# Rounding the query and output weights ahead, and four smaller moves, in a fused decoder block

## The chip, the cores and the metric

The kernel runs on one core of a Trainium2 chip. The metric is device time in microseconds for one execution. Of the kernel before there are three runs, with a median of 2021.86 us, from 2018.86 to 2024.74. A difference of under 0.3%, some 6 us, can't be told from no change by such runs.

Five engines work at the same time, each through its own list of instructions, in order: TensorE (PE: matrix products and transposes), VectorE (DVE), ScalarE (ACT), GpSimd (POOL) and SyncE (SP), which here only issues transfers between DRAM and on-chip memory. ScalarE can issue transfers too. Engines wait for one another through semaphores.

## The reference

One layer of a decoder over 1024 tokens of width 1024, in 32-bit floats, all shapes fixed:

```python
h = h + 0.5 * swiglu(rms_norm(h, ffn1_norm[l]), ffn1_w_gu[l], ffn1_w_down[l])
h = h + hybrid_mixer(rms_norm(h, mix_norm[l]), w_in[l], ..., w_out[l])
h = h + 0.5 * swiglu(rms_norm(h, ffn2_norm[l]), ffn2_w_gu[l], ffn2_w_down[l])
...
return rms_norm(h, final_norm)
```

`swiglu` multiplies by a gate-and-up matrix (1024 x 5504), takes silu(gate) * up, and multiplies by a down matrix (2752 x 1024). `hybrid_mixer` multiplies the normed rows by `w_in`, splits the columns, and runs two groups of heads beside each other:

```python
parts = jnp.split(h @ w_in, IN_SPLITS, axis=-1)
nq, k_c, v_c, k_s, v_s, k_w, v_w, gl, hq, hf, hi, hg = parts
o_nsa = nsa_group(nq, k_c, v_c, k_s, v_s, k_w, v_w, gl, ...)
o_hg = hgrn2_group(hq, hf, hi, hg, lower_bound, hg_norm)
return jnp.concatenate([o_nsa, o_hg], axis=-1) @ w_out
```

`nsa_group` is attention with 8 heads of width 64 in 2 groups that share keys and values. Each query attends in three ways, each with its own softmax and gate: to compressed blocks of keys, to selected blocks of 64 keys (of which here all are chosen, 16 of 16), and to a window of 512 keys. The compressed keys and values come from `gelu(flat @ w1) @ w2` over overlapping blocks of 32 rows (`cmp_k_w1` and `cmp_v_w1` are 2048 x 256). `hgrn2_group` is a gated linear recurrence with 4 heads of width 128 in chunks of 64 rows.

## The kernel before

**Numbers.** TensorE multiplies a rounded form of 32-bit floats here. To keep precision, an operand is split into a rounded high part and the remainder, and a product is three matmuls: high x high, high x low, low x high (`mm3`, L162 to L164). The split (`split`, L151) takes the high part on GpSimd (L154) or as a copy on ScalarE (L156), and the remainder by a subtraction on VectorE (L158). So every weight that enters a product first is loaded and then costs one rounding and one subtraction of 128x512.

**Order.** The program goes through first feed-forward, mixer, second feed-forward and final norm. Most work is written as Python generators whose steps are called in turn, so that dense products lie between the steps of latency-bound work. Instructions are then put in order engine by engine by priority; `late()` (L119) makes what is recorded inside it stand behind the last instructions so far recorded of ScalarE, GpSimd, VectorE and SyncE.

**The product after the up-projection.** `down` (L653) multiplies the hidden rows by the down matrix in a Strassen form of seven stages. A stage goes over 11 slices m of the contraction, and each slice is twelve matmuls of 128x512 (L683 to L685). For each slice a hidden piece `hr` and a weight piece `raw` are loaded (`dr`) and split into `hh, hl` (high part on ScalarE, L706) and `dh, dl` (high part on GpSimd, L707), all named `dw`. Stages 0, 2 and 3 end with `copies` (L670): four copies on ScalarE empty the four PSUM banks into `hk` or `q`, and the next stage's matmuls write into the same banks.

**The mixer** (loop from L1466). Compression (`compress`, L942) runs beside the four recurrence heads and the key and value projection. It loads `w1` in 16 pieces of 256 KB (L987, SyncE; four buffers) and multiplies (L990), keys first, then values. `hgrn_unit` (L830) is one half of one head: its last steps scale the rows to `o4` (L921, VectorE), and after one `yield` (L923) transposes them (L926). `wo_split` (L311) loads `w_out` in 16 pieces beside this (L321), splits them (high part on GpSimd) and writes both parts to DRAM (L325); `wq_tile` reads them back for the output projection.

**Attention** goes over 8 blocks qb of 128 queries and 2 groups g, four heads each, so 16 groups of heads. For each head `att_soft` (L1127) makes scores (L1148, L1149, against the high part `ka` and the low part `kl` of the keys), reduces them (L1154), takes exponentials on ScalarE (L1191), reciprocals on VectorE (L1193) and scales the rows on GpSimd (L1195, three branches). `att_pv` (L1200), called in steps during the next group's heads, transposes the scaled rows P of all four heads (L1225), splits them into `ph` on ScalarE (L1227) and `pt` on VectorE (L1228), and multiplies by the values (L1216). Between the heads lie dense steps: the query projection (`att_proj_q`, L1046, three matmuls a step) and, in the second half, the output projection. Its weights are tiles of 128 columns made by `wtile`: load, high part on GpSimd, remainder on VectorE. Keys are made for half of the rows at a time by `att_kv` (L1103: `ka` L1122 on ScalarE, `kl` L1125 on VectorE). Before each head's rest the loop calls `next(dense, None)` five times in the first group, where nothing else fills TensorE, and once in the others (L1535); what is left after the first half is run at L1555.

**The tail.** `finish` (L1681) norms and writes each block of 128 output rows, in two transfers of 512 columns.

Of the kernel before, what the change touches and what calls it, by code (L numbers as in the profile page):

```python
# [21 lines left out]
KT = D // 128  # L22
# [49 lines left out]
class Net:  # L72
# [238 lines left out]
    def wo_split(self, p, spill):  # L311

        nc = self.nc
        self.wo = {}
        for cq in range(4):
            src = self.wsrc("w_out", cq)
            for kp in range(4):
                t = p.tile([128, 1024], F32R, name=self.nm("wo"), tag="fl", bufs=2)
                lo, hi = t[:, :512], t[:, 512:]
                raw = lo.bitcast(F32)  # L320
                nc.sync.dma_start(out=raw.rearrange("p (k c) -> p k c", k=2), in_=src[:, 2 * kp:2 * kp + 2])  # L321
                self.split(hi, lo, raw)
                yield
                page = self.wo[cq, kp] = spill.tile([128, 1024], F32, name=self.nm("wo"), tag="wo", bufs=16)
                nc.sync.dma_start(out=page[:], in_=t[:].bitcast(F32))  # L325

# [326 lines left out]
    def down(self, pool, pool2, name, H, h, scale, final, after=(), wide=None, tail=0):  # L653
# [20 lines left out]
        later = {}  # L674
        for n, (an, bn) in enumerate(stages):
# [11 lines left out]
            for m in range(11):  # L687
# [18 lines left out]
                self.split(hh, hl, hr[:], "act")  # L706
# [123 lines left out]
    def hgrn_unit(self, p, t, half, states, mo):  # L830
# [92 lines left out]
        yield  # L923
# [18 lines left out]
    def compress(self, p, hg, sp, raw):  # L942
# [33 lines left out]
        for n, _ in enumerate(fls[0]):  # L976
            if n % 2:
                yield
        for s in range(2):
            w1 = self.i["cmp_v_w1" if s else "cmp_k_w1"][0].rearrange("(i p) c -> p i c", p=128)  # L980
# [4 lines left out]
            for i in range(0, 16, 2):  # L985
                w1t = p.tile([128, 2, 256], F32, name=self.nm("w1"), tag="kr", bufs=4)
                nc.sync.dma_start(out=w1t[:], in_=w1[:, i:i + 2, :])  # L987
                for ii in range(2):
                    for m in range(2):
                        mm(hb[m][:, :126], w1t[:, ii, m * 128:m * 128 + 128], fl[s][i // 8][:, i % 8 + ii, :, :],  # L990
# [55 lines left out]
    def att_proj_q(self, p, wp, x, half, tag, tiles=range(4)):  # L1046

        nc = self.nc
        for i in tiles:
            g, m = i // 2, i % 2  # L1050
            w = wp(i)
            yield w
            b = self.bank(tag)
            for kt in range(KT):
                self.mm3(b[:], w[0][kt], w[1][kt], x[0][kt // 2][half][:, kt % 2, :], x[1][kt // 2][half][:, kt % 2, :],
# [71 lines left out]
    def att_soft(self, p, g, qb, hh):  # L1127
# [13 lines left out]
        st = p.tile([128, 12], F32, name=self.nm("sm"), tag="sm", bufs=8)  # L1141
# [47 lines left out]
        def rest():  # L1189
# [3 lines left out]
            nc.vector.reciprocal(out=st[:, 6:9], in_=st[:, 6:9])  # L1193
# [3 lines left out]

# [67 lines left out]
def body(ctx, tc, ins, out):  # L1265
# [189 lines left out]
    if True:  # L1455
# [65 lines left out]
        for half in range(2):  # L1521
# [33 lines left out]
            if half == 0:  # L1555
                for _ in dense:
                    pass
# [158 lines left out]
```

## Time and profile before

| What | Value |
|---|---|
| Median of 3 runs | 2021.86 us (2018.86 to 2024.74) |
| Profiled execution, its own time | 2021.49 us |
| Its span, first to last instruction | 2019.8 us |
| TensorE busy | 1980.2 us (98%), 10862 matmuls |
| VectorE busy | 1410.7 us (70%) |
| ScalarE busy | 781.5 us (39%) |
| GpSimd busy | 524.8 us (26%) |
| Mean granted TensorE clock | 0.996 |
| DMA | 294.34 MB, mean 146 GB/s |

The rows come from one profiled execution. Times in them count from the start of its span. A matmul counts as busy from its start to its modelled end, so matmuls that overlap in the pipeline each show more than their share: one of 128x512 shows 0.39 us. Register, branch, semaphore and transfer-issuing instructions are not counted as busy; issues of transfers are shown as SPq and ACTq. The line numbers are those of the kernel before.

### The profile page before, as it was taken

How to read it: one execution, taken by the hardware profiler on the slowest of the kernel's cores; microseconds unless marked ns; L12 is line 12 of the kernel's file. 1: busy time of each engine (PE TensorE's matmuls, PEld its weight loads, DVE VectorE, ACT ScalarE, POOL GpSimd, SP SyncE). 2: the span in 40 equal slices, each digit the busy share in tenths (PEclk: the TensorE clock that was granted, in tenths of full speed). 3: DMA queues.
4: the chain of work that ended last, by engine and by line, in shares of the span. 5: the costliest groups of instructions: out<-in, count | busy, mean ns of one | idle time of the engine just before them, and what ended most of it. 6: DMA issues, size and time to landing. Idle time of an engine off the chain costs nothing.

```text
span 2019.8 us, 31101 instructions
## 1 busy us (share of the span) xinstructions
PE 1980.2 (98%) x10862; PEld 1660.5 (82%) x10862; DVE 1410.7 (70%) x2881; ACT 781.5 (39%) x1649; POOL 524.8 (26%) x624
## 2 busy tenths in 40 slices
PE   9999999999999999999989999999999999999998
PEld 6888888888788888889877788888888888888886
DVE  5987778668756557756468888746867677558677
ACT  5533233322323322222368767645433333223233
POOL 2133233234421012100146433301222122113221
PEclk9999999999999999999999999999999999999999
DMA  5346666258753245200001012462446666147663
GB/s 188 119 131 200 217 218 218 96 180 280 238 186 126 73 131 192 86 24 33 27 22 58 14 66 69 152 214 84 141 168 213 208 220 203 67 173 251 210 191 141
DMA packets 153789, 294.34 MB, mean 146 GB/s; under 512 B 17280, under 2 KB 38816, under 8 KB 153632
## 3 DMA queue, kind: packets, MB, share of 16 engines
q1 hardware_dynamic: 147488, 279.23, 41.2%
q10 hardware_dynamic: 6144, 13.12, 1.8%
q8 instruction: 86, 1.41, 0.3%
q14 instruction: 71, 0.58, 0.1%
HBM read 207.88 MB, written 84.41 MB: 145 GB/s over the span
## 4 chain that ended last, share of the span: by engine, by line
PE 87%; DVE 5%; ACT 3%; issue 3%; DMA 1%; POOL 1%; ACTq 0%; SPq 0%; DVEq 0%; POOLq 0%
PE b L162 16%; PE b L164 16%; PE b L163 16%; PE b L683 7%; PE b L684 7%; PE b L685 7%; PE b L745 3%; PE b L746 3%; PE b L747 3%; PE b L1216 3%; PE b L1225 2%; PE b L841 2%; ACT P L1191 1%; PE b L1149 1%; PE b L1148 1%
## 5 line engine op out<-in xcount | busy, mean ns | idle before, releaser
L163 PE MATMUL b<-xT,wp 128*128 128x512 f32 x1196 | 466.3, 390 | 1.6 <-DVE xT L379 1.5
L162 PE MATMUL b<-xT,wp 128*128 128x512 f32 x1196 | 466.4, 390 | 1.2 <-ACT xT L378 0.7
L164 PE MATMUL b<-xT,wp 128*128 128x512 f32 x1196 | 465.9, 390 | 0.0
L158 DVE TENSOR_TENSOR dw<-dr,dw 128x512 fp32r<-128x512 f32 x308 | 239.4, 820 | 101.1 <-ACT dw L156 87.7
L162 PEld LDWEIGHTS b<-xT,wp 128*128 128x128 f32 x1196 | 224.6, 188 | 50.6 <-POOL wp L154 1.7
L163 PEld LDWEIGHTS b<-xT,wp 128*128 128x128 f32 x1196 | 224.6, 188 | 49.6 <-DVE xT L379 3.4
L164 PEld LDWEIGHTS b<-xT,wp 128*128 128x128 f32 x1196 | 224.6, 188 | 47.2 <-DVE wp L158 0.6
L683 PE MATMUL b<-dw,dw 128*128 128x512 f32 x616 | 240.6, 391 | 4.2 <-ACT q L670 2.9
L685 PE MATMUL b<-dw,dw 128*128 128x512 f32 x616 | 240.2, 390 | 0.2 <-DVE dw L158 0.2
L684 PE MATMUL b<-dw,dw 128*128 128x512 f32 x616 | 240.0, 390 | 0.0
L154 POOL TENSOR_SCALAR dw<-dr 128x512 fp32r<-128x512 f32 x154 | 123.4, 808 | 283.4 <-PE b L685 172.1
L156 ACT ACTIVATE wp<-ws 128x512 fp32r<-128x512 f32 x148 | 93.3, 632 | 252.7 <-PE b L163 241.3
L156 ACT ACTIVATE dw<-dr 128x512 fp32r<-128x512 f32 x154 | 94.1, 629 | 246.0 <-PE b L683 135.0
L1195 POOL TENSOR_SCALAR P<-P,sm,gate 128x64 f32<-128x64 f32 (+8 forms) x192 | 126.4, 672 | 147.9 <-DVE sm L1193 127.1
L683 PEld LDWEIGHTS b<-dw,dw 128*128 128x128 f32 x616 | 115.7, 188 | 29.5 <-ACT q L670 3.4
L158 DVE TENSOR_TENSOR wp<-ws,wp 128x512 fp32r<-128x512 f32 x148 | 110.3, 747 | 41.1 <-ACT wp L156 40.9
L685 PEld LDWEIGHTS b<-dw,dw 128*128 128x128 f32 x616 | 115.7, 188 | 25.2 <-DVE dw L158 1.4
L684 PEld LDWEIGHTS b<-dw,dw 128*128 128x128 f32 x616 | 115.7, 188 | 23.6
L156 ACT ACTIVATE wp<-wr 128x512 fp32r<-128x512 f32 x115 | 72.2, 629 | 154.8 <-PE b L163 133.8
L1191 ACT ACTIVATE P<-P,sm 128x64 f32<-128x64 f32 (+8 forms) x192 | 114.9, 600 | 36.3 <-DVE sm L1154 35.0
L475 POOL TENSOR_TENSOR ws<-wr 128x512 f32<-128x512 f32 x37 | 49.6, 1341 | 299.1 <-DVE wp L158 257.5
L1228 DVE TENSOR_TENSOR pt<-b,ph 128x512 fp32r<-128x512 f32 x148 | 99.2, 688 | 30.0 <-ACT ph L1227 29.1
(302 smaller groups left out, 3906.5 us busy)
## 6 DMA issues: line engine op xcount, KB each, us to landing
dr<-hs SPq DMA_DIRECT2D x242, 256.0 KB, 3.1
wr<-in_ffn_w_gu_dram SPq DMA_DIRECT2D x82, 512.0 KB, 4.0
hs<-hk SPq DMA_DIRECT2D x140, 256.0 KB, 3.7
hs<-wd SPq DMA_DIRECT2D x88, 256.0 KB, 3.1
wd<-in_ffn_w_down_dram SPq DMA_DIRECT2D x84, 256.0 KB, 3.4
dr<-in_ffn_w_down_dram SPq DMA_DIRECT2D x62, 256.0 KB, 4.4
wq<-wo SPq DMA_DIRECT2D x40, 256.0 KB, 3.7
wr<-in_w_in_dram SPq DMA_DIRECT2D x16, 512.0 KB, 4.3
```

Of the source, the lines that this page charges most:

```text
L154: nc.gpsimd.tensor_scalar(out=hi, in0=src, scalar1=1.0, scalar2=1.0, op0=OP.mult, op1=OP.mult)
L156: nc.scalar.activation(out=hi, in_=src, func=AF.Copy)
L158: eng.tensor_tensor(out=lo, in0=src, in1=hi.bitcast(F32), op=OP.subtract)
L162: mm(ps, wh, xh, start=first, stop=False, skip_group_check=skip)
L163: mm(ps, wh, xl, start=False, stop=False, skip_group_check=skip)
L164: mm(ps, wl, xh, start=False, stop=last, skip_group_check=skip)
L683: mm(bs[t][:], hl[:, c], dh, start=first, stop=False, skip_group_check=True)
L684: mm(bs[t][:], hh[:, c], dh, start=False, stop=False, skip_group_check=True)
L685: mm(bs[t][:], hh[:, c], dl, start=False, stop=last, skip_group_check=True)
L1191: nc.scalar.activation(out=rng[br], in_=rng[br], func=AF.Exp, scale=-1.0, bias=m, accum_out=st[:, 6 + br:7 + br])
L1195: nc.gpsimd.tensor_scalar(out=rng[br], in0=rng[br], scalar1=st[:, 6 + br:7 + br], scalar2=self.gate[:, qb, h * 3 + br:h * 3 + br + 1], op0 ...
L1228: nc.vector.tensor_tensor(out=l[:w], in0=b[:w], in1=h[:w].bitcast(F32), op=OP.subtract)
```

## The change

1. `wo_split` becomes `presplit`: 24 pieces in place of 16, the first eight being the four query weight tiles. A piece is loaded one step ahead, and after the `yield` its split is put late, with the high part on ScalarE. The query tiles are written to DRAM (`wqs`), and attention reads both parts back by `wqtile`, two transfers of 512 KB, where `wtile` loaded and split seven times.
2. In `down` the `hh, hl` splits for m > 1 of the stage after a set of copies are put behind the last copy.
3. The `w1` pieces of the compression are loaded from ScalarE's queue, three pieces ahead, each late.
4. `hgrn_unit` yields three times before the last transposes.
5. In attention the reciprocals of two heads are taken in one instruction, and the scaling of both follows it. Four dense steps go between heads in the first group (without the empty one a tile that they had before), three in the second; what is left is run before the last group of the first half, where the first group's keys of the second half are now made; the second group's follow at block 4.
6. At the tail blocks 4 to 6 write both halves from SyncE, and block 7 its first half from ScalarE.

```diff
+            with self.late():
+                self.split(hi, lo, lo.bitcast(F32), "act")
+            if n == 4:
+                if k == 0:
+                    self.wqs[key[1]] = spill.tile([128, 2, 2, 512], F32, name=self.nm("ws"), tag="wqs", bufs=4)
+                nc.sync.dma_start(out=self.wqs[key[1]][:, :, k, :], in_=t[:].bitcast(F32).rearrange("p (a c) -> p a c", a=2))
...
+    def wqtile(self, pool, i, bufs=1):
+
+        h, l = (pool.tile([128, KT * self.WW], F32R, name=self.nm(t), tag=t, bufs=bufs)[:, :1024] for t in ("wh", "wl"))
+        for k, w in ((1, h), (0, l)):
+            self.nc.sync.dma_start(out=w.bitcast(F32).rearrange("p (b c) -> p b c", b=2), in_=self.wqs[i][:, k])
...
-                self.split(hh, hl, hr[:], "act")
+                with self.tc.issue_after(behind) if behind and m > 1 else nullcontext():
+                    self.split(hh, hl, hr[:], "act")
...
+            behind = None
             if n in (0, 2, 3):
                 x = copies(bs, "q" if n else "hk")
+                behind = nc.cur_bb.bb.instructions[-1]
...
-        yield
+        for _ in range(3):
+            yield
         b = self.bank("b")
...
+            t = w1t[s, i] = p.tile([128, 2, 256], F32, name=self.nm("w1"), tag="kr", bufs=4)
+            with self.late():
+                nc.scalar.dma_start(out=t[:], in_=w1[:, i:i + 2, :])
...
-            nc.vector.reciprocal(out=st[:, 6:9], in_=st[:, 6:9])
+            if hh % 2 == 0:
+                return
+            nc.vector.reciprocal(out=both[:, :, 6:9], in_=both[:, :, 6:9])
+            scaled(h - 1, both[:, 0, :], *before)
+            scaled(h, st, rng)
...
-                    if qb == 4:
-                        net.att_kv(kp1, 1, (g,), wf)
+                    if qb == 3 and g:
+                        for _ in dense:
+                            pass
+                        cv.close()
+                        kp1 = pool(cv, "k1", "right")
+                        net.att_kv(kp1, 1, (0,), wf)
+                    if qb == 4 and g:
+                        net.att_kv(kp1, 1, (1,), wf)
...
-                        for _ in range(1 if pv else 5):
+                        for _ in range(1 + (qb == 0) * (3 - g)):
...
-            (nc.sync if i and tt >= 4 else nc.scalar).dma_start(out=out[0, tt * 128:(tt + 1) * 128, k], in_=y[:, k])
+            (nc.sync if 4 <= tt < 7 or tt == 7 and i else nc.scalar).dma_start(out=out[0, tt * 128:(tt + 1) * 128, k], in_=y[:, k])
```

Where the instructions stand is shown at three places. The first is ScalarE at the end of the third stage of the first `down`: `dw` are high parts that are made from loaded pieces `dr`, `q` are the copies of the banks `b`. Before:

```order
L156 ACTIVATE dw_4909<-dr_4906 128x512
L156 ACTIVATE dw_4935<-dr_4932 128x512
L156 ACTIVATE dw_5015<-dr_5012 128x512
L156 ACTIVATE dw_5038<-dr_5035 128x512
L156 ACTIVATE dw_4829<-dr_4826 128x512
L156 ACTIVATE dw_4856<-dr_4853 128x512
L670 ACTIVATE q_4770<-b_4484 128x512
L670 ACTIVATE q_4771<-b_4485 128x512
L670 ACTIVATE q_4772<-b_4486 128x512
L670 ACTIVATE q_4773<-b_4487 128x512
```

And in the changed kernel:

```order
L156 ACTIVATE dw_4728<-dr_4725 128x512
L691 ACTIVATE q_4770<-b_4484 128x512
L691 ACTIVATE q_4771<-b_4485 128x512
L691 ACTIVATE q_4772<-b_4486 128x512
L691 ACTIVATE q_4773<-b_4487 128x512
L156 ACTIVATE dw_4829<-dr_4826 128x512
L156 ACTIVATE dw_4884<-dr_4881 128x512
L156 ACTIVATE dw_4909<-dr_4906 128x512
L156 ACTIVATE dw_4935<-dr_4932 128x512
L156 ACTIVATE dw_4856<-dr_4853 128x512
```

The pieces 4829, 4856, 4884, 4909, 4935, 5015 and 5038 have moved from ahead of the four copies to behind them.

The second is TensorE at the end of the first head of the recurrence: L745 to L747 (now L769 to L771) are dense matmuls of the next head's projection, `ident,f` are the transposes of the scaled rows. Before:

```order
L747 MATMUL b_7265<-wh_7073,xT_5681 128x256
L926 MATMUL b_7293<-ident,f_6250 128x128 x4
L926 MATMUL b_7299<-ident,f_6334 128x128 x2
L745 MATMUL b_7307<-wh_7073,xT_5682 128x256
L746 MATMUL b_7307<-wl_7074,xT_5682 128x256
```

And in the changed kernel:

```order
L771 MATMUL b_7263<-wh_7072,xT_5681 128x256
L769 MATMUL b_7293<-wh_7072,xT_5682 128x256
...
L771 MATMUL b_7326<-wh_7072,xT_5689 128x256
L951 MATMUL b_7354<-ident,f_6250 128x128 x4
L951 MATMUL b_7360<-ident,f_6340 128x128 x4
```

Two more banks of dense matmuls, `b_7293` and `b_7326` with 24 each, now stand ahead of the transposes.

The third is the queue of the last `w1` pieces of the compression. `wr` are weight tiles of 512 KB for the recurrence, `wo` the pieces of `wo_split`. On SyncE before:

```order
L987 DMA w_1316_6659<-in_cmp_v_w_dram 128x2x256
L987 DMA w_1317_6665<-in_cmp_v_w_dram 128x2x256
L987 DMA w_1318_6671<-in_cmp_v_w_dram 128x2x256
L301 DMA wr_7457<-in_w_in_dram 128x4x256
L987 DMA w_1319_6677<-in_cmp_v_w_dram 128x2x256
L321 DMA wo_6748<-in_w_out_dram 128x512
L301 DMA wr_7458<-in_w_in_dram 128x4x256
```

And on ScalarE in the changed kernel, where `g` and `v` are evacuations of the recurrence and `hid` the activation of the compression:

```order
L851 ACTIVATE v_6499<-b_6616 128x128
L1011 DMA w_1316_6644<-in_cmp_v_w_dram 128x2x256
L1011 DMA w_1317_6651<-in_cmp_v_w_dram 128x2x256
L1011 DMA w_1318_6658<-in_cmp_v_w_dram 128x2x256
L1011 DMA w_1319_6665<-in_cmp_v_w_dram 128x2x256
L1032 ACT_TABLE_LOAD
L1032 ACTIVATE hid_6683<-b_6606 128x126
```

The last four pieces have left the queue of the `wr` tiles and stand behind one evacuation on ScalarE.

## Rows read from the trace of the kernel before

**Rows 1.** The page's busy time, share of the span and instructions of each engine.

```profile
PE 1980.2 (98%) x10862; PEld 1660.5 (82%) x10862; DVE 1410.7 (70%) x2881; ACT 781.5 (39%) x1649; POOL 524.8 (26%) x624
```

**Rows 2.** TensorE's waits: line, what ended them, us in total, times, longest.

```profile
PE b L1216 <- ACT ph L1227: 4.3, 9, 0.9
PE b L683 <- ACT q L670: 2.9, 1, 2.9
PE b L990 <- DMA w<-in_cmp_v_w_dram: 2.9, 2, 1.6
...
PE b L926 <- DVE f L921: 2.5, 1, 2.5
PE b L162 <- POOL wh L154: 2.0, 2, 1.2
PE b L1148 <- ACT ka L1122: 1.6, 1, 1.6
...
PE b L1225 <- POOL P L1195: 0.7, 1, 0.7
```

**Rows 3.** Busy time by stretch: PE, PEld, DVE, ACT, POOL, clock, DMA share, GB/s.

```profile
500.00:550.00 50.00, 47.06 (x207) 38.23 (x206) 39.09 (x58) 15.64 (x31) 23.36 (x30) 1.00 0.76 237
...
850.00:900.00 50.00, 50.00 (x501) 44.62 (x501) 30.02 (x103) 11.16 (x41) 3.14 (x4) 1.00 0.11 35
...
1000.00:1050.00 50.00, 43.69 (x212) 34.95 (x211) 26.28 (x109) 27.94 (x93) 17.09 (x38) 0.95 0.06 21
...
1095.90:1114.00 18.10, 16.90 (x93) 12.79 (x91) 15.45 (x46) 13.85 (x38) 12.31 (x19) 1.00 0.45 147
```

**Rows 4.** The same view, two stretches at half clock.

```profile
799.40:802.80 3.40, 3.40 (x19) 3.40 (x18) 0.69 (x1) 0.85 (x2) 0.74 (x2) 0.52 0.44 142
...
1035.00:1038.40 3.40, 3.40 (x13) 3.01 (x12) 1.03 (x4) 1.20 (x3) 0.63 (x2) 0.50 0.31 111
```

**Rows 5.** Timeline (start, length, instruction, idle before) at the third stage's end.

```profile
528.05 0.39 PE L685 MATMUL b<-dw,dw 128*128 128x512 f32 x1
531.39 0.50 PE L683 MATMUL b<-dw,dw 128*128 128x512 f32 x1 [2.94 <-ACT q L670]
...
530.76 2.04 ACT L670 ACTIVATE q<-b 128x512 f32<-128x512 f32 x4
```

**Rows 6.** Timeline of the end of the value compression: TensorE, ScalarE, SyncE's queue.

```profile
735.65 3.73 PE L990 MATMUL b<-fl,w 128*128 128x126 f32 x32
740.62 2.05 PE L990 MATMUL b<-fl,w 128*128 128x126 f32 x16 [1.24 <-DMA w<-in_cmp_v_w_dram]
...
745.92 1.16 PE L990 MATMUL b<-fl,w 128*128 128x126 f32 x8 [1.63 <-DMA w<-in_cmp_v_w_dram]
...
736.48 0.28 ACT L827 ACTIVATE v<-b 128x128 f32<-128x128 f32 x1 [0.36 <-DVE g L826]
...
739.05 0.37 SPq L301 DMA_DIRECT2D wr<-in_w_in_dram  x1
739.51 0.46 SPq L987 DMA_DIRECT2D w<-in_cmp_v_w_dram  x1
```

**Rows 7.** Transfers issued from 690 to 760 us: KB each, median us to landing.

```profile
w<-in_cmp_v_w_dram SPq DMA_DIRECT2D x8, 256.0 KB, 3.0
```

**Rows 8.** The page's costliest groups: two operations of a split (busy, mean ns).

```profile
L156 ACT ACTIVATE wp<-ws 128x512 fp32r<-128x512 f32 x148 | 93.3, 632 | 252.7 <-PE b L163 241.3
...
L158 DVE TENSOR_TENSOR wp<-ws,wp 128x512 fp32r<-128x512 f32 x148 | 110.3, 747 | 41.1 <-ACT wp L156 40.9
```

**Rows 9.** Timeline of scaling on GpSimd and the transposes that read it.

```profile
1086.44 1.68 POOL L1195 TENSOR_SCALAR P<-P,sm,gate 128x384 f32<-128x384 f32 x3 [2.33 <-DVE sm L1193]
...
1098.81 1.89 POOL L1195 TENSOR_SCALAR P<-P,sm,gate 128x512 f32<-128x512 f32 x3 [1.41 <-DVE sm L1193]
...
1088.74 1.04 PE L1225 MATMUL b<-ident,P 128*128 128x128 f32 x8
...
1101.95 1.09 PE L1225 MATMUL b<-ident,P 128*128 128x128 f32 x8
```

More of the change, by code (lines that the diff above doesn't have):

```diff
@@ L673, in down @@
         stages = (("A11", "B11"), ("A12", "B21"), ("S2", "T2"), ("S3", "T3"), ("A22", "T4"), ("S1", "T1"), ("S4", "B22"))
-        later = {}
+        later, behind = {}, None
         for n, (an, bn) in enumerate(stages):
@@ L978, in compress, with load @@
                 yield
+        w1t, loads = {}, [(s, i) for s in range(2) for i in range(0, 16, 2)]
+        def load():
+            s, i = loads.pop(0)
+            w1 = self.i["cmp_v_w1" if s else "cmp_k_w1"][0].rearrange("(i p) c -> p i c", p=128)
+            t = w1t[s, i] = p.tile([128, 2, 256], F32, name=self.nm("w1"), tag="kr", bufs=4)
+            with self.late():
+                nc.scalar.dma_start(out=t[:], in_=w1[:, i:i + 2, :])
+        for _ in range(3):
+            load()
         for s in range(2):
-            w1 = self.i["cmp_v_w1" if s else "cmp_k_w1"][0].rearrange("(i p) c -> p i c", p=128)
             w2 = self.i["cmp_v_w2" if s else "cmp_k_w2"][0].rearrange("(m p) c -> p m c", p=128)
@@ L1140, in att_soft @@
         P2 = p.tile([128, 704], F32, name=self.nm("P2"), tag="P2", bufs=8)
[L1141 removed]
+        if hh % 2 == 0:
+            self.st = p.tile([128, 2, 12], F32, name=self.nm("sm"), tag="sm", bufs=4)
+        both = self.st
+        st = both[:, hh % 2, :]
         lo = max(0, qb - 4)
@@ L1498, in body @@
             wf = pool(ck, "wf")
-            dense = net.att_proj_q(qp, lambda i: net.wtile(wp, "w_in", ("q", i)), X, 0, "b", (0, 1))
+            wq = {i: net.wqtile(wp, i, 2) for i in range(2)}
+            dense = net.att_proj_q(qp, wq.get, X, 0, "b", (0, 1))
             next(dense)
             net.att_kv(kp0, 0)
-            wq = {2: net.wtile(wf, "w_in", ("q", 2), None, 1, (wp, 128, "wr", 2))}
+            wq[2] = net.wqtile(wf, 2)
             for _ in dense:
@@ L1507, in body, with turn @@
         banks(a=4, b=2, o=1, w=1)
-        load = lambda i: net.wtile((wf, wp)[i % 2], "w_in", ("q", i), None, 1, (sp2, 128, "pt", 5))
-        wq[3] = load(3)
-        dense = chain(net.att_proj_q(qp, wq.get, X, 0, "b", (2, 3)),
-                      net.att_proj_q(qp, lambda i: wq[3] if i == 3 else load(i), X, 1, "w", (3, 0, 1, 2)))
+        wq[3] = net.wqtile(wp, 3)
+        def turn(half, i):
+            w, n = wq[i], {(0, 3): 0, (1, 0): 1, (1, 1): 2}.get((half, i))
+            if n is not None:
+                wq[n] = net.wqtile((wf, wp)[n % 2], n)
+            return w
+        dense = chain(net.att_proj_q(qp, lambda i: turn(0, i), X, 0, "b", (2, 3)),
+                      net.att_proj_q(qp, lambda i: turn(1, i), X, 1, "w", (3, 0, 1, 2)))
         M = [[[None, None] for _ in range(4)] for _ in range(2)]
```

54 lines of the change are left out of this document (28 added, 26 removed).

## The prediction, made before the changed kernel was run

> **What bounds the kernel now.** I read the busy shares first. TensorE is busy for 1980.2 us of a span of 2019.8, VectorE for 70% of it, ScalarE 39%, GpSimd 26% [rows 1]. So only the 39.6 us in which TensorE shows no matmul, and time lost to its clock, can be had by moving other engines' work. Next the list of TensorE's waits: it names the places, and most of those that the change touches occur once or twice in the whole program [rows 2]. Then busy time by stretch. Over 850 to 900 us, where the four-head recurrence runs, TensorE is busy for 50.00 of 50 us while ScalarE has 11.16 and VectorE 30.02; in 1000 to 1050, where attention begins, it is busy for 43.69 at a clock of 0.95; and in the group of heads between 1095.9 and 1114.0 it has 16.90 of 18.1 us and VectorE 15.45 [rows 3]. The clock is the last thing. Right after a gap it falls to half, the 1.2 GHz level, for some 3.4 us: 0.52 from 799.4 and 0.50 from 1035.0 [rows 4]; a third such stretch follows the GpSimd wait at 1048 and is part of the 0.95. Each costs half of 3.4, that is 1.7 us. So the question is not how much work leaves an engine but whether each named wait goes, and what is late next.
>
> **The change part by part.** The sum is made against the profiled execution, 2021.49 us: its span and 1.69 around it; the median of the runs is 2021.86, 0.37 more.
>
> *Roundings behind the copies in the up-projection.* At the end of the third stage TensorE issues its last matmul at 528.05 and the next at 531.39 after a wait of 2.94 us; the four copies that empty the banks start only at 530.76 [rows 5]. In the order the roundings of seven later hidden pieces stand between the last matmul and these copies on ScalarE, each waiting for its load. After the change they stand behind. The copies can start when the last matmul is done, as four copies of 0.51 us take 2.04 for all and the first one frees the first bank. What becomes late is the rounding of those seven pieces, but the first two of a stage are not moved and a piece feeds twelve matmuls at 0.227 each (47.06 us for 207 [rows 3]), 2.7 us, against one rounding of 0.63 [rows 8]. The wait goes: -2.9. Bounds: -2.9, and 0 if a load is the next thing to come late. The other stage ends show no such wait, so I count nothing there.
>
> *Compression weights.* The last products of the value compression run as 3.73 us, 2.05 us and 1.16 us, with waits of 1.24 and 1.63 us for loads between them [rows 6]. The load that ends the second wait was issued at 739.51, behind the issue of a large weight tile at 739.05 on the same queue [rows 6]; it lands at 745.92, 6.4 us later, where the median landing is 3.0 [rows 7]. On ScalarE's queue it stands behind nothing large. Against a gain speaks a rule of the Trainium skill (Trainium Kernel Development and Optimization, Key Constraints): transfers issued from SyncE, ScalarE and GpSimd share the same 16 DMA engines, so that another issuer saves only issue time; by that alone this part would give nothing, and the sum would be 1.6 higher. The rows show more than issue time: a load that is issued in order behind a large one, and lands twice as late. I go by the rows, with this limit: the last four loads now come in order after ScalarE's evacuation at 736.48 [rows 6], so the first of them is issued at about 736.8 and lands at 739.8. The three pieces ahead of it keep TensorE busy from 735.65 for 3 x 0.93 (3.73 for four), to 738.45: a wait of about 1.4 takes the place of the 1.24. Then four more pieces, 3.7 us, and the seven dense matmuls that now lie between, 1.6: the end is at 745.2 instead of 746.83. So -1.6; bounds -2.9 (both waits go) and 0 (landing as slow as in the second wait).
>
> *Three steps instead of one before the transposes of the recurrence.* One wait of 2.5 us for VectorE [rows 2], and behind it the half-clock stretch from 799.4 [rows 4]. In the new order 48 small matmuls stand ahead of these transposes (second piece of the order), about 5.8 us at the pace of the rows around it, twice the gap. The wait goes (-2.5) and with it the cause of the slow stretch (-1.7): -4.2. Bounds: -4.2 and -2.5 if the clock falls there anyway. The other three heads show no wait, so nothing there.
>
> *The early roundings themselves.* 24 roundings on ScalarE at 0.63 us are 15.1 us, where GpSimd had 16; VectorE has 8 more at 0.75, 6.0 us, less the 14 that leave attention [rows 8]. They lie in the recurrence, where TensorE has 50.00 of 50 and the other two have 39 and 20 us of each 50 free [rows 3]: nothing. If that cover is gone, 21 us. The query weights are written out and read back as they are needed: two transfers of 512 KB in place of a load and roundings. The read for the second tile can start only when the last key matmul has freed its buffer; the large tile's 6.4 us (739.51 to 745.92 above) against the 24 matmuls, 5.4 us, that stand before it leaves up to 1 us of wait. I take +0.5, bounds 0 and +1.
>
> *Attention.* Waits that go: for GpSimd's rounding of a query weight 2.0, two times [rows 2]; for the second half's keys 1.6 [rows 2], since these are now made a group earlier. The second group of heads gets nine matmuls a head in place of three, 24 more in all, 5.4 us, exactly where TensorE starves: of the nine waits for ScalarE's copies (4.3 us in all [rows 2]) I put a third, 1.5 us, just behind this group (an estimate), and there lies the slow stretch from 1035.0 [rows 4]. I count -1.5, -1.7, and -1.7 for the slow stretch behind the vanished GpSimd wait: with 2.0 and 1.6 these are -8.5. Against it: the dense steps run out before the last group of the first half, which loses 30 matmuls, 6.8 us. There TensorE has 16.90 and VectorE 15.45 of 18.1 [rows 3]; without the 6.8 TensorE has 10.1 and VectorE sets the pace. The group can't get shorter than about 15.4, so of the 6.8 moved only 18.1 - 15.4 = 2.7 is won back there: +4.1. And the reciprocals of two heads are taken together, so the first head's scaling on GpSimd waits for the second's and the second's ends three operations later, 1.68 to 1.89 us. At two groups the scaling ends at 1088.12 and 1100.70, and TensorE's transposes that read it start at 1088.74 and 1101.95 [rows 9]: slack of 0.62 and 1.25, so waits of 1.1 and 0.6 come. Later groups have more. With two or three more places like these I take +2.5; bounds 0 and +7 (nine early groups at 0.8). Together -8.5 + 4.1 + 2.5 = -1.9; bounds -8 and +4.
>
> *The tail.* One output transfer's issue leaves ScalarE and another is added to SyncE; an issue takes 0.37 [rows 6]. I count 0, bounds -0.4 and +0.4.
>
> Sum: -2.9 - 1.6 - 4.2 + 0.5 - 1.9 = -10.1, so 2021.49 - 10.1 = 2011.4. The median would lie 0.4 higher; I say **2011.5**.
>
> **The rivals.** *Attention gives it back* (no change that can be told). For it: no filler in the group from 1095.9 and the one behind it, and paired scaling, both in the stretch where TensorE already waits. Against it: three waits and two slow stretches there lose their cause. Price: attention at its bound of +4 and the load term at +1, with the three other parts at -8.7: 2021.5 - 3.7 = 2017.8. Chance 0.13.
>
> *The paired scaling decides* (slower). If the scaling of the last pair ends TensorE's wait in every one of the 16 groups by three operations of 0.6, 1.9 us, this is 30 us, in place of the 2.5 counted: 2011.4 + 27.5 = 2039. From 0.8 us a group on (12.6 us over 16) it eats all that the rest gives. For it: the slack of 0.62 and 1.25 above [rows 9]. Against it: only one wait of 0.7 us for GpSimd's P in the whole trace [rows 2], and the slack grows towards the later groups, whose head takes longer. Chance 0.05.
>
> *The moves bite less than they say.* At the third stage's end the next load takes the place of the copies, and the value compression waits as long on another queue: -4.2 + 0.5 - 1.9 is left, 2015.9. (For the compression this is what the rule of the Trainium skill named above would bring.) For it: the load's own 3 us after the evacuation. Against it: the ScalarE order alone explains the wait at 530.76. Chance 0.12.
>
> *Attention goes all the way*: the filler takes the idle time and the pairs fit the slack, -8 instead of -1.9: 2005.3. Chance 0.22.
>
> **How the numbers follow.** My forecast has 0.48, the others 0.13, 0.05, 0.12 and 0.22, as given. A difference under 0.3% of the median, 6 us, can't be told from no change: faster is under 2015.8, slower above 2027.9. Faster takes my own case, the best one and half of the case at 2015.9, 0.76, less 0.01 for the upper end of my own: 0.75. Same has 0.20, slower 0.05. The range reaches from 2003 (the best case with compression and load at their good ends) to 2019 (attention gives it back, and a little more).
>
> **What would show it.** Right: no wait for the copies at the end of the third stage; one wait in the value compression instead of two; no gap ahead of the four transposes and a clock of 1.00 from 800 to 850; no wait for GpSimd's weights or for the keys; in the group before the second half TensorE idle for some 4 us more than now. Wrong: waits for GpSimd's P in many groups; the loads of the rounded query weights ending a wait of over 1 us; ScalarE's roundings in the waits of the recurrence. My time is wrong by more than the range if attention as a whole gets longer by over 6 us, or shorter by over 10.

## The result, and the profile after

The changed kernel takes 2007.64 us (median of four runs), against 2023.3 us for the kernel before (four runs): 0.9923 of its time, 95% interval 0.9905 to 0.9941. That is faster, by 15.7 us or 0.8%, where 10.4 were forecast (2011.5). The profiled execution has a span of 2005.8 us against 2019.8, which is 14.0 less, and this is what the traces can account for. (One of the four runs took 3275.66 us at a granted clock of 0.556 and is left out of the ratio; without it the median is 2007.51.)

The busy times answer to [rows 1]:

```profile
PE 1976.2 (99%) x10862; PEld 1661.2 (83%) x10862; DVE 1390.7 (69%) x2843; ACT 793.1 (40%) x1673; POOL 501.7 (25%) x594
```

TensorE runs the same 10862 matmuls, busy 4 us less, in part since two stretches at half clock are left of three; its idle time falls from 39.6 to 29.6 us. VectorE is relieved of 20 us and GpSimd of 23, and ScalarE has 12 more.

Where the time went is read best from the start of the same matmul in both timelines:

| Place (start of the first matmul unless said) | before | after | gained so far |
|---|---|---|---|
| first down product | 438.22 | 437.60 | 0.62 |
| its fourth stage | 531.39 | 527.47 | 3.92 |
| compression | 698.39 | 694.28 | 4.11 |
| compression, last matmul | 746.80 | 741.81 | 5.00 |
| attention, first scores | 1008.94 | 1001.41 | 7.54 |
| first transposes of block 5, group 0 | 1191.67 | 1177.55 | 14.12 |
| second down product | 1800.14 | 1786.03 | 14.11 |
| last matmul | 2010.55 | 1996.17 | 14.38 |
| end | 2019.77 | 2005.78 | 13.99 |

So 3.5 us come from the down product (from 0.62 to 4.11), 0.9 from the compression, 2.5 from the recurrence, 6.6 from attention; 0.4 are lost in the tail, and the 0.6 ahead of everything lie where nothing was changed.

TensorE's waits, in the columns of [rows 2]:

```profile
PE b L1269 <- POOL P L1238: 4.9, 6, 1.3
PE b L1260 <- ACT ph L1271: 2.6, 6, 0.7
PE b L162 <- issue: 2.4, 1, 2.4
PE b L1025 <- DMA w<-in_cmp_v_w_dram: 2.1, 1, 2.1
...
PE b L1185 <- DVE sm L1191: 1.1, 3, 0.6
...
PE b L1186 <- DVE kl L1159: 0.5, 1, 0.5
```

The waits for the copies `q`, for the recurrence's `f`, for GpSimd's `wh` and for the keys `ka` are gone. A new one stands on top: 4.9 us, six times, for the scaled rows P from GpSimd. The compression has one wait instead of two.

The third stage's end, to be held against [rows 5]: ScalarE's copies, then TensorE's matmuls, the last of the third and the first three of the fourth stage among them.

```profile
525.63 2.64 ACT L691 ACTIVATE q<-b 128x512 f32<-128x512 f32 x4 [13.43 <-PE b L706]
528.16 2.71 ACT L156 ACTIVATE dw<-dr 128x512 fp32r<-128x512 f32 x5
...
527.24 0.39 PE L706 MATMUL b<-dw,dw 128*128 128x512 f32 x1
527.47 0.39 PE L704 MATMUL b<-dw,dw 128*128 128x512 f32 x1
527.69 0.39 PE L705 MATMUL b<-dw,dw 128*128 128x512 f32 x1
```

ScalarE waits for the banks now, not the banks for ScalarE: the copies start bank by bank as each is finished, and TensorE goes on without a gap. The roundings follow behind.

The end of the value compression, against [rows 6]: TensorE, ScalarE's queue, SyncE's queue.

```profile
731.54 2.84 PE L1025 MATMUL b<-fl,w 128*128 128x126 f32 x24
735.30 3.20 PE L1025 MATMUL b<-fl,w 128*128 128x126 f32 x24
740.56 1.67 PE L1025 MATMUL b<-fl,w 128*128 128x126 f32 x8 [2.06 <-DMA w<-in_cmp_v_w_dram]
...
732.44 2.35 ACTq L1011 DMA_DIRECT2D w<-in_cmp_v_w_dram  x4
...
734.94 0.37 SPq L301 DMA_DIRECT2D wr<-in_w_in_dram  x1
...
736.18 0.37 SPq L301 DMA_DIRECT2D wr<-in_w_in_dram  x1
```

The last four loads are issued from 732.44 to 734.8, all ahead of the two large tiles on the other queue (between these two SyncE issues a 256 KB piece of the early roundings as well). Still the last one lands only at about 740.5, some 6 us after its issue, and TensorE waits 2.06 us for it.

Busy time by stretch, with the clock in the eighth place, against [rows 3] and [rows 4]:

```profile
500.00:550.00 50.00, 50.00 (x222) 41.27 (x221) 36.15 (x57) 14.71 (x29) 19.18 (x29) 1.00 0.68 222
800.00:850.00 50.00, 50.00 (x494) 43.40 (x494) 36.61 (x100) 15.79 (x50) 5.37 (x6) 1.00 0.39 138
...
1000.00:1050.00 50.00, 45.58 (x233) 37.11 (x233) 27.98 (x128) 32.28 (x111) 17.09 (x39) 0.97 0.20 64
741.00:744.40 3.40, 3.40 (x13) 2.92 (x12) 0.00 (x0) 2.49 (x4) 0.00 (x0) 0.51 0.61 208
1003.90:1007.30 3.40, 2.93 (x7) 2.39 (x8) 0.67 (x3) 1.44 (x3) 0.00 (x0) 0.50 0.00 0
```

The early roundings cost nothing where they now lie (50.00 of 50 from 800 to 850 with ScalarE at 15.79). The half-clock stretch of 799.4 is gone, but one stands behind the compression's wait, at 741.0; the two in attention (1035.0 and 1048.7) are gone too, and one has come at its start, 1003.9.

### The profile page after: what moved, and what is told of

It is laid out like the page before. It is cut to its first block, busy times and chain, and to the rows that moved or that the text cites. A ratio compares the mean times of both kernels' runs of the same rounds, so it can differ in the third digit from the quotient of the medians.

```text
span 2005.8 us, 30977 instructions
## 1 busy us (share of the span) xinstructions
PE 1976.2 (99%) x10862; PEld 1661.2 (83%) x10862; DVE 1390.7 (69%) x2843; ACT 793.1 (40%) x1673; POOL 501.7 (25%) x594
## 4 chain that ended last, share of the span: by engine, by line
PE 93%; DVE 3%; ACT 1%; POOL 1%; issue 1%; DMA 1%; SPq 0%; DVEq 0%; ACTq 0%; POOLq 0%
PE b L162 17%; PE b L163 16%; PE b L164 16%; PE b L706 7%; PE b L704 7%; PE b L705 7%; PE b L769 3%; PE b L771 3%; PE b L770 3%; PE b L1269 3%; PE b L1260 3%; PE b L865 2%; PE b L1185 1%; PE b L1186 1%; POOL P L1238 1%
## 5 line engine op out<-in xcount | busy, mean ns | idle before, releaser
L158 DVE TENSOR_TENSOR dw<-dr,dw 128x512 fp32r<-128x512 f32 x308 | 234.5, 809 | 74.3 <-ACT dw L156 61.5
```

Source lines behind the costliest of these rows:

```text
L158: eng.tensor_tensor(out=lo, in0=src, in1=hi.bitcast(F32), op=OP.subtract)
```

## The experiments

Each kernel is the changed one but for the edit shown (one is the kernel before). Its time is the median; how its parts lie is read from the same places as in the table above. "In attention" means from the first scores to the first transposes of block 5: 182.73 us before, 176.14 after. The kernel before was timed again beside each batch: 2021.27 us (experiments 1 to 4), 2023.64 (5 to 8), 2021.06 (9 to 11) and 2023.04 (12), against the 2023.3 of the result. So medians of one kernel differ by up to 2.6 us between batches, and where a difference is of that size the places in the traces decide.

**1. The roundings back in front of the copies.**

```diff
-                with self.tc.issue_after(behind) if behind and m > 1 else nullcontext():
+                with nullcontext():
                     self.split(hh, hl, hr[:], "act")
```

> The changed kernel, but the roundings of the hidden pieces in the down product stand where they stood before (no order behind the four copies). Theory A (ScalarE's order alone made the wait): the wait of about 2.9 us for the copies comes back at the end of the third stage of the first down product, everything ahead of it and behind it keeps its time, and the whole is 2.9 to 3.5 us longer than the changed kernel. Theory B (the wait hung on when the loads of that one execution landed): no wait over 1 us there, the whole within 1 us.

Measured: 2010.53 us, 2.9 over the changed kernel (held against the kernel before, it gains 10.7 us instead of 15.7). The wait for the copies is back:

```profile
PE b L704 <- ACT q L691: 1.6, 1, 1.6
```

The gap is 1.6 us in this execution (2.9 in that of before), and to the fourth stage's first matmul 2.5 us are lost; the kernel of experiment 7, whose order at this place is that of before, has 1.7. So the order makes the wait, as theory A has it, but its size varies from one execution to another; that this hangs on when the loads for the roundings in front land is likely and not shown.

**2. The compression's loads back on SyncE's queue, each ahead of its own products.**

```diff
...
-                if loads:
-                    load()
+                w1t[s, i] = p.tile([128, 2, 256], F32, name=self.nm("w1"), tag="kr", bufs=4)
+                nc.sync.dma_start(out=w1t[s, i][:], in_=w1[:, i:i + 2, :])
```

> The changed kernel, but the compression's w1 pieces are loaded from SyncE's queue, each just ahead of its own products, as before. Theory A (the move brought little here, since the last piece still lands late beside the large weight tiles, and its one wait of 2.1 us sets off a half-clock stretch): two waits of some 1.2 and 1.6 us, no half-clock stretch behind them, the whole within 1 us of the changed kernel or up to 1 us shorter. Theory B (the queue was the cause and the move gains): the whole 1 to 2.9 us longer.

Measured: 2006.62 us, 1.0 under the changed kernel, which is within the spread of either. There are two waits, 2.3 us in all, the longer 1.4:

```profile
737.12 2.05 PE L1016 MATMUL b<-fl,w 128*128 128x126 f32 x16 [0.82 <-DMA w<-in_cmp_v_w_dram]
742.22 1.16 PE L1016 MATMUL b<-fl,w 128*128 128x126 f32 x8 [1.43 <-DMA w<-in_cmp_v_w_dram]
```

The compression takes 47.80 us against 47.53, and no half-clock stretch follows. In this pair of executions the move to another queue is worth nothing: theory A. More executions are compared further down.

**3. One step instead of three ahead of the recurrence's last transposes.**

```diff
-        for _ in range(3):
-            yield
+        yield
         b = self.bank("b")
```

> The changed kernel, but with one step instead of three ahead of the recurrence's last transposes. Theory A (the gap is cut by the steps, and with it the half-clock stretch behind it): a wait of some 2.5 us for VectorE ahead of the first head's transposes and half clock behind it, the whole 2.5 to 4.2 us longer. Theory B (the early roundings on ScalarE instead of GpSimd already free VectorE there): no wait over 0.5 us, the whole within 0.5 us.

Measured: 2005.44 us. The only wait that is left there:

```profile
PE b L950 <- DVE f L945: 0.3, 1, 0.3
```

From the last compression product to the first scores it takes 259.68 us, against 258.36 to 258.42 in experiments 5 and 9 to 12, which have the three steps, the same code up to there, and no half-clock stretch in it either. So three steps are worth 1.3 us here, about a third of a microsecond a head, and not the gap of 2.5: the wait is as theory B says, the time fits neither. The profiled execution (2005.91 us) was not longer than the changed kernel's, since the compression's last load landed in time in it, without any wait.

**4. Each head scaled at once.**

```diff
-            if hh % 2 == 0:
-                return
-            nc.vector.reciprocal(out=both[:, :, 6:9], in_=both[:, :, 6:9])
-            scaled(h - 1, both[:, 0, :], *before)
+            nc.vector.reciprocal(out=st[:, 6:9], in_=st[:, 6:9])
             scaled(h, st, rng)
```

> The changed kernel, but each head takes its own reciprocals and is scaled on GpSimd at once, as before. Theory A (the pairing makes TensorE wait for GpSimd, six times, 4.9 us): these waits shrink to under 1 us in all and the whole is 2 to 4.9 us shorter. Theory B (those waits only stand where others would, for ScalarE's and VectorE's copies): they shrink, but waits for the copies grow by as much, and the whole is within 1 us. Theory C (32 reciprocals more on VectorE cost more than the waits): the whole 1 to 5 us longer.

Measured: 1999.88 us, 0.9893 of the kernel before (0.9876 to 0.9910) and 7.8 under the changed one (21.4 us gained on the kernel before instead of 15.7): the best of all. TensorE waits for P nowhere. Attention takes 170.11 us, 6.0 less, of which 1.7 are a half-clock stretch that this execution doesn't have. How the wait arises in the changed kernel (GpSimd's scaling, then the transposes that read it, first group of block 2):

```profile
1064.62 3.33 POOL L1238 TENSOR_SCALAR P<-P,sm,gate 128x384 f32<-128x384 f32 x6 [0.63 <-DVE sm L1232]
...
1065.68 0.49 PE L1269 MATMUL b<-ident,P 128*128 128x128 f32 x3
1066.98 0.77 PE L1269 MATMUL b<-ident,P 128*128 128x128 f32 x5 [0.81 <-POOL P L1238]
```

The six operations in a row are the last pair's and end at 1067.95. Transposes go head by head, and the fourth reads the last head, whose scaling now stands behind the three operations of the head before it: TensorE stops after three transposes. With each head scaled at once the last head's group is three operations:

```profile
1060.15 1.68 POOL L1235 TENSOR_SCALAR P<-P,sm,gate 128x384 f32<-128x384 f32 x3
...
1063.36 1.68 POOL L1235 TENSOR_SCALAR P<-P,sm,gate 128x384 f32<-128x384 f32 x3 [0.65 <-DVE sm L1230]
```

Theory A, and more in the whole than its range. The 32 reciprocals that the pairing saves are not worth the 4 to 6 us that it costs in attention.

**5. Fewer dense steps in the second group of heads.**

```diff
-                        for _ in range(1 + (qb == 0) * (3 - g)):
+                        for _ in range(1 + (qb == 0) * (1 - g) * 3):
```

> The changed kernel, but the second group of heads gets one dense step a head, as before, instead of three; the eight steps (24 matmuls, 5.4 us) that are left run together just ahead of the last group of the first half. Theory A (the steps fill idle time where attention begins): waits of some 1.5 to 3 us for ScalarE's and VectorE's copies come back between the second and the fourth group, and the whole is 2 to 5 us longer. Theory B (where the steps lie does not matter, only that the weights come rounded): the whole within 1 us.

Measured: 2006.85 us; attention 177.30, 1.2 longer, with two half-clock stretches in it where the changed kernel has one. Theory B, as it seems; but the waits for P shrink from 4.9 to 1.9 us, since the lump of 24 matmuls hides some of them. Experiment 12 does this without the pairing.

**6. One step, and the early roundings on GpSimd.** The edit of experiment 3, and:

```diff
-                self.split(hi, lo, lo.bitcast(F32), "act")
+                self.split(hi, lo, lo.bitcast(F32))
```

> The changed kernel with one step ahead of the recurrence's last transposes, and the early roundings of query and output weights on GpSimd instead of ScalarE (still a step late, query weights included). Theory A (the gap of 2.5 us went since the weights are rounded a step late, so that VectorE no longer waits for a load and a rounding in the middle of the recurrence's chain): no wait over 0.5 us ahead of the transposes, the stretch of the recurrence as long as in the changed kernel within 1 us. Theory B (it went since ScalarE rounds instead of GpSimd): a wait of 1 to 2.5 us is back.

Measured: 2006.78 us (one run). Two waits for `f`, 0.7 in all, the longer 0.5; from the last compression product to the first scores it takes 261.15 us, 1.5 more than with ScalarE in experiment 3, and as much more than in the changed kernel with its half-clock stretch. So it is the load a step ahead and the rounding a step late that took the big gap away, not the engine: theory A in the wait, though the stretch is longer than it said.

**7. The kernel before, with three steps.** The edit of experiment 3 the other way round, in the kernel before.

> The kernel before, with nothing changed but three steps instead of one ahead of the recurrence's last transposes. Theory A (the steps alone are enough too): the wait of 2.5 us ahead of the first head's transposes is gone, the attention's first scores start 2.5 us earlier, or 4.2 where the half-clock stretch goes with it. Theory B (the late roundings alone did it): the wait stays, over 1 us.

Measured: 2016.23 us (one run). The eight transposes come without a gap, where [rows 2] has 2.5 us:

```profile
798.91 1.04 PE L927 MATMUL b<-ident,f 128*128 128x128 f32 x8
```

From the last compression product to the first scores it takes 257.72 us, against 262.14 before: 4.42 us, the gap and the half-clock stretch. Theory A. Either of the two parts removes the gap; where the late roundings are there already, the steps are worth 1.3 (experiment 3).

**8. Scaling at once, loads inline, the tail as before**: the edits of experiments 2 and 4, and

```diff
-            (nc.sync if 4 <= tt < 7 or tt == 7 and i else nc.scalar)
+            (nc.sync if i and tt >= 4 else nc.scalar)
```

> The changed kernel with each head scaled at once, the compression's pieces on SyncE's queue each ahead of its products, and the output transfers of the tail as before: three of the parts undone. If the parts add up, -5 for the scaling (with the waits for GpSimd gone), -1 for the compression (two short waits and no half clock), -0.4 for the tail (the stretch from the last matmul to the end 9.2 us instead of 9.6): some 6 us under the changed kernel, 2001. If the pairing and the compression share their gain (the half-clock stretch behind the compression is only moved): some 4.5 us under it.

Measured: 2001.43 us, 0.9893 (0.9877 to 0.9911), 6.2 under the changed kernel, and the same as experiment 4 alone. The tail, from the start of the last matmul to the end, takes 9.23 us as it did before (9.61 in the changed kernel): 0.4. A wait of 1.5 us for a query tile that is read back is there now, and eats the rest:

```profile
PE b L164 <- DMA wl<-ws: 1.5, 1, 1.5
```

The next four have each head scaled at once, and are held against experiment 4 (170.11 us in attention).

**9. Query tiles of attention split there again.**

```diff
-        wq[3] = net.wqtile(wp, 3)
+        wq[3] = net.wraw(wp, 3, sp2)
...
-                wq[n] = net.wqtile((wf, wp)[n % 2], n)
+                wq[n] = net.wraw((wf, wp)[n % 2], n, sp2)
```

(`wraw` is `wtile` as attention used it before.)

> The changed kernel with each head scaled at once, and with the four query tiles that are taken up during attention loaded raw and split there again, as before (eight roundings of 128x512 on GpSimd, eight subtractions on VectorE); the early copies of them are still made. To be compared with the kernel in which only the scaling is undone, whose attention takes 170.1 us from the first scores to the first transposes of the first group of block 5. Theory A (leaving these splits out of attention is worth what they take on VectorE, where it sets the pace, and the GpSimd waits of 2.0): 5 to 9 us longer there. Theory B (only the two GpSimd waits went): 2 to 3.7 us longer.

Measured: 2003.86 us; attention 173.12, 3.0 longer. No wait for GpSimd's `wh` is named: the tiles are taken up one tile ahead here, and before they were not. So the 3.0 lie in the range of theory B, but not for its reason. What is left is the price of the work itself, as theory A has it, at less than its size; experiment 10 tries this on VectorE alone.

**10. Eight idle subtractions on VectorE.**

```diff
+            for _ in range(2 * ((half, i) not in ((0, 2), (1, 3)))):
+                scratch = sp2.tile([128, 512], F32R, name=net.nm("sc"), tag="pt", bufs=5)
+                nc.vector.tensor_tensor(out=scratch[:], in0=net.dwin[:, :512], in1=net.dsel[:, :512], op=OP.subtract)
```

> The same kernel (each head scaled at once), with eight subtractions of 128x512 added on VectorE at the places where a new query tile begins; they wait for nothing, their result is not used. Theory A (VectorE sets the pace in the early groups): most of their 8 x 0.7 = 5.6 us shows, 3 to 5.6 us longer in attention. Theory B (VectorE has slack beside TensorE): under 1 us.

Measured: 2004.03 us; attention 174.70, 4.6 longer, of which 1.7 are a half-clock stretch at 1002.9. The subtractions (line, operation, count, busy us, mean ns) are

```profile
L1557 DVE TENSOR_TENSOR sc<-dwin,dsel 128x512 fp32r<-128x512 f32 x8 | 5.6, 710 | 2.9 <-PE b L1185 2.8
```

so that 4.6 - 1.7 = 2.9 of 5.6 us show: between the theories. (The 2.9 in the row is something else: VectorE's idle time just ahead of these instructions, nearly all ahead of the first, which started with the first scores.) About half of VectorE's work there is on the path, and this is as much as experiment 9 costs. (They also take turns in the five `pt` buffers; the two effects were not parted.)

**11. The first keys of the second half at block 4 again.**

```diff
-                        net.att_kv(kp1, 1, (0,), wf)
-                    if qb == 4 and g:
-                        net.att_kv(kp1, 1, (1,), wf)
+                    if qb == 4:
+                        net.att_kv(kp1, 1, (g,), wf)
```

> The same kernel (each head scaled at once), but the first group's keys of the second half are made where they are first used, at block 4, as before. Theory A (the wait for the keys was worth its length): a wait of 1.6 us for ScalarE's part is back, 1.5 to 2 us longer. Theory B (it only stands where VectorE would be late anyway): within 0.5 us.

Measured: 2000.69 us; attention 170.38, 0.3 longer, no wait for `ka`. Theory B: the wait of 1.6 us does not come back with the place of the keys alone.

**12. Experiment 5 with each head scaled at once.**

> The changed kernel with each head scaled at once, and with one dense step a head in the second group of heads, as before, instead of three (the eight steps left, 5.4 us of matmuls, run together ahead of the last group of the first half). Compared with the kernel in which only the scaling is undone, 170.1 us from the first scores to the first transposes of block 5. Theory A (the early steps fill idle time; with the paired scaling the lump only hid it under waits that were there anyway): 3 to 6 us longer, waits for ScalarE's and VectorE's copies in the second to fourth group. Theory B (it does not matter where the steps lie): within 1 us.

Measured: 2002.71 us; attention 172.82, 2.7 longer, 1.7 of it a half-clock stretch at 1024.9. One us is for the steps themselves; between the theories. The stretch follows a wait of 0.93 us for ScalarE's copy at 1024.3 that the steps had filled; the kernel before has the same wait at 1034.6 and experiment 5 at 1026.7, and the clock falls behind it there too (experiment 7 has it at 1029.7, and the clock does not fall).

## Why the prediction was right, and where it was not

The time lies in the range, and on the side that was forecast, 3.9 us under the point. Step by step:

- *Roundings behind the copies*: -2.9 forecast; 3.5 gained between the first matmul of the product and the compression. Right in place and mechanism: the copies lead, the loads did not become the next thing late. Experiment 1 gives 2.5 at this place. A gap costs a little more than the idle time that is shown for it: from 528.05 to 531.39 [rows 5] are 3.34 us from start to start where 0.23 is the pace, and the next matmul starts another 0.34 later. That the wait was 2.9 long in the execution that the sum was made from, and 1.6 and 1.7 in two others with this order, could not be known from one trace.
- *Compression*: -1.6 forecast, -0.9 came, and a half-clock stretch of 1.7 behind it takes that back. The step that failed is the landing time. I took the 3.0 us of [rows 7] for a load that "stands behind nothing large" on its queue; it landed after 6. (The wait of 1.4 us that I put ahead of the first of the four did not come: the dense matmuls stood there, not behind the four.) In the executions with loads on ScalarE's queue the last piece's wait is 2.1, 2.0, 0, 2.9, 1.7, 0.7, 2.1, 1.5, 2.1 and 1.2 us (changed kernel, experiments 1, 3 to 6 and 9 to 12), 1.6 on average; on SyncE's the two waits sum to 2.9, 2.3, 2.1 and 2.1 (before, 2, 7, 8), 2.4 on average. So the order in one queue did not make the late landing; what SyncE's queue (q1) moves meanwhile goes with it. While that load was under way, q1 moved (packets, MB, share of the 16 engines) in experiment 3, where it landed after 3.7 us, and in experiment 4, after 6.9:

```profile
q1 hardware_dynamic: 122, 0.12, 12.7%
```

```profile
q1 hardware_dynamic: 977, 1.09, 49.4%
```

  The instructions up to there are the same in both. From its first to its last product the compression takes 46.8 us on average over the ten executions and 47.9 over the four; the half-clock stretch behind it in three of the ten takes half a microsecond of this back on average. So some 0.6 us is left of the 1.6, which no median here can show. The rule that I named and did not follow (the Trainium skill, Trainium Kernel Development and Optimization, Key Constraints: transfers issued from SyncE, ScalarE and GpSimd run on the same 16 DMA engines) would have given nothing for this part. The traces agree with the sharing: the same load took 3.7 or 6.9 us as q1 had 12.7% or 49.4% of the engines' time beside it.
- *Three steps*: -4.2 forecast; 2.5 gained from the last compression product to the first scores, and 4.2 if the slow stretch at 741, which belongs to the compression, is set apart. Right in its sum. But the gap had two sufficient cures in the same change (experiments 3, 6 and 7), and I had looked only at one. VectorE, in order, stood in the middle of the chain to `f` behind a subtraction that waited for GpSimd's rounding, which waited for its load (kernel before, VectorE and GpSimd):

```profile
796.19 0.69 DVE L158 TENSOR_TENSOR wo<-wo 128x512 fp32r<-128x512 f32 x1 [0.86 <-POOL wo L154]
...
797.97 1.13 DVE L921 SCALAR_TENSOR_TENSOR f<-b,hr,g 128x128 f32<-128x128 f32 x4
...
795.54 0.62 POOL L154 TENSOR_SCALAR wo<-wo 128x512 fp32r<-128x512 f32 x1 [1.59 <-DMA wo<-in_w_out_dram]
```

- *Early roundings*: nothing forecast, nothing lost (50.00 of 50). The read of the second tile: +0.5 forecast; no wait here, 1.5 in experiment 8, over the bound of 1. (The 6.4 us from 739.51 to 745.92 behind that bound are of the 256 KB load, not of a large tile.)
- *Attention*: -1.9 forecast, -6.6 came, nearer to the rival *Attention goes all the way* (-8) than to my own case, and not for that rival's reason: the pairs did not fit the slack. The waits for `wh` (2.0) and the keys (1.6) went, those for ScalarE's copies `ph` fell from 4.3 to 2.6 us, and two half-clock stretches went while one came. Three other terms were wrong and partly cancel. First, "+4.1", that the last group of the first half would starve without dense steps. It did not. From the first transposes of block 3, group 0, to those of block 4, group 0, the time is (before, then after)

```profile
1101.95:1145.47 43.52, 39.23 (x222) 30.20 (x220) 37.73 (x103) 31.99 (x78) 23.16 (x31) 1.00 0.12 41
```

```profile
1093.57:1129.62 36.05, 32.56 (x197) 26.02 (x195) 31.38 (x96) 30.14 (x75) 20.84 (x30) 1.00 0.08 26
```

  7.5 us less, for 25 recorded matmuls less; TensorE's idle time falls from 4.3 to 3.5 us. I had held VectorE's 15.45 us for a floor, but VectorE lost work there as well (37.73 to 31.38 us). And by the loop 27 matmuls were left there, not 30, as one of the steps is the empty one with which a tile begins; only nine of them belong to the four heads of the group, and the other 18 ran behind it. Of the 7.5 us, 24 matmuls at 0.227 make 5.4 and the vanished wait for the keys 1.6. Second, the price of the pairing: "+2.5", measured 4.9 of waits and some 4.3 to 6.0 of time (experiment 4), the rival's mechanism in the early groups alone. Third, the splits that leave attention stand nowhere in its sum, but for the waits for `wh`; they are worth 3.0 (experiment 9; experiment 10 makes VectorE's part plausible).
- *The tail*: 0 forecast, +0.4 came, its upper bound.

Of the rivals, the paired scaling was the nearest to a danger: without it the gain is 21.4 us (2021.27 to 1999.88, experiment 4) instead of 15.7. It stayed in the groups up to block 4. One of my signs of being wrong came with it in part (waits for GpSimd's P, six of them), and one of the signs of being right did not (TensorE some 4 us more idle in the group before the second half). That the sum still came within 3.9 us is in part luck: the compression and the three steps gave 2.4 us less than forecast, or 0.7 with the half-clock stretch set apart, and attention 4.7 more.

What stays open: the parts that were undone one by one in attention give 3.0 (splits), 0.3 (keys), and 2.7 (steps, half clock included), 6.0 together, where the kernel without pairing gains 12.6 us over the one before. One half-clock stretch (1.7) and the two waits for `wh` (2.0), which the query tile taken up a tile ahead removes in any of these kernels, make 9.7. Where the time lies on TensorE can be counted: its busy time in attention, before and in experiment 4, is

```profile
1008.94:1191.67 182.73, 168.93 (x958) 136.90 (x957) 145.78 (x504) 132.78 (x373) 90.54 (x152) 0.98 0.13 41
```

```profile
1003.00:1173.11 170.11, 163.19 (x958) 134.57 (x956) 139.69 (x498) 132.50 (x374) 86.67 (x146) 1.00 0.16 51
```

The idle time falls from 13.8 to 6.9 us, and two half-clock stretches of 1.7 go: 10.3 of the 12.6. The last 2.3 us lie in the busy time of the same number of matmuls. Which part of the change gave the idle time that no experiment returned was not found.

## What to carry to other kernels

Merging two small operations holds up the work on the first result. Where that work then stands ahead of the last link of a chain, the consumer of the last result pays: count what the last result waits for, not what the engine does in all. A list of waits shows the places of a gain, but a gap may have more than one cure, and undoing each part against the changed kernel and doing it alone in the old one tells which are worth keeping. Work on an engine that is not the bottleneck can still be worth half its length: VectorE is busy for 139.69 of 170.11 us in attention (experiment 4), and 5.6 us more of it cost 2.9 (experiment 10).

## What was not expected of the hardware

The same gap does not always bring the slow clock. TensorE's wait of 2.4 to 2.6 us at the start of attention is in all 14 executions; a half-clock stretch of 3.4 us follows it in five (changed kernel, experiments 3, 5, 7 and 10) and not in the others. Behind the compression's single wait it came at 2.1, 2.0 and 2.9 us (changed kernel, experiments 1 and 4), not at 2.1 in experiments 9 and 11. Nor does the length decide: in the kernel before the longest gap, 2.94 us at 531.39, is followed by full clock, and one of 0.86 us at 1048.39 by half. So 1.7 us a gap is a chance, not a price, and comparisons of single executions have to be corrected for it.

A load of 256 KB that was issued half a microsecond ahead of two of 512 KB and one of 256 KB on another queue landed between 3.7 and 6.9 us after its issue (experiments 3 and 4), with the same instructions up to there.
